# Three edits between attention and ffn_down of a hybrid decoder layer: where the last projections' operands lie, how the sums for ffn_up are formed, in which pieces the residual is loaded

## The chip, the core and the metric

The kernel runs on one core of a Trainium2 chip as one program. Its time is the device time of one launch in microseconds (us), smaller is better. TensorE (PE) multiplies into PSUM, VectorE (DVE) and ScalarE (ACT) read PSUM and SBUF, GpSimd (POOL) reads SBUF, and SyncE (SP) issues every transfer from its one queue, in order. Each engine works through its own list of instructions in order and waits at semaphores for the others.

## What is computed

One decoder layer over 1024 tokens of width 1024 in float32, cut here to the parts that the change touches:

```python
x = x + jnp.concatenate([o_nsa, o_gdn], axis=-1) @ w_out[l]
h = rmsnorm(x, norm_ffn[l])
u = causal_dwconv(h @ ffn_up[l], ffn_conv[l])
gate, up = jnp.split(u, 2, axis=-1)
x = x + (jax.nn.silu(gate) * up) @ ffn_down[l]
return rmsnorm(x, norm_final)
```

o_nsa comes from sparse attention (8 heads, 2 key heads), o_gdn from a gated delta rule (4 heads of 128). ffn_up is 1024 x 5632, ffn_down 2816 x 1024.

## The kernel before

**Numbers.** Every float32 operand of a matmul is split into a high part (an ACT copy to fp32r) and a low part (the operand minus the high part, on DVE or POOL), and a product is three matmuls: high x high, high x low, low x high. The moving operand is 128x512, one PSUM bank.

**Order of work.** The whole program is unrolled. A planner walks it with its own estimate of times and lays out one list for each engine: of what is ready it takes what comes first in the text, unless `tc.issue_after` ties an instruction behind another of its engine. So instructions stand in the lists in another order than in the text, and the lists of a changed kernel can differ far from the change. Tiles lie in pools. Pools are stacked from the left or the right end of SBUF in the order in which they are opened; a pool that comes to lie over bytes of closed pools waits until all users of these pools are done, or, with `reuse_waits="tile"`, each tile waits only for the tiles whose bytes it takes. Inside a pool a tag has `bufs` buffers that are used in turn.

**Phases.** `phase_in` (norm, input projections, the gated delta rule; its last projections are those of `evac_k`, whose split weights lie in pool wk). `phase_attend` runs attention in 16 units, one for each of 8 tiles of 128 tokens (order 7, 6, ..., 0) and 2 key heads: `select` (tile pc), `scores` (tiles p_win and p_sel), `values` (transposes pt, operands ph and pl, sums po), one unit in each of three stages at a time; between their steps the matmuls of `out_gdn` and `out_nsa` are woven in as fillers. `out_gdn` multiplies o_gdn with its half of w_out for all tiles, adds x and stores to x1 in DRAM (d_x1). `out_nsa` does the other half for the four tiles 7 to 4 that are finished early; its operands are the two buffers of tag mg in pool og (mg holds high and low part side by side, 8 KB for two; og's own tag 4 KB). `nsa_norm` norms a finished tile into K.mix.

**`phase_out`** (lines 1020 to 1054) goes over tiles 7 to 4, whose x1 is loaded again (line 1033), and 3 to 0, whose projection is still to be done: the cast mh (line 1037), the low part ml on DVE (line 1040), the residual x_res (line 1042), 24 matmuls out_ps into two banks, the sum with x_res (line 1048), a store. mh, ml and x_res lie in pool xo, which takes bytes of attention's pools. After the first four tiles `norm_transpose` norms and transposes the rows, 32 transposes in eight groups k, and `put_parts` writes the high and low part of group k: D[0] for k below 4, D[1] above.

**`norm_second`** (lines 1063 to 1124) does the same for tiles 3 to 0. ffn_up is computed with Winograd's form of Strassen's product: seven quarter products for eight, with sums of quarters. With the activations' quarters A11 = D[0], A12 = D[1] (the first half of tiles), A21 and A22 = D[2] (the second half), T[2] = A22 - A21, T[0] = A21 - A11 and T[1] = A22 - A21 + A11, T[3] = A12 - T[1]. `put` forms A22 - A21 (s1) in one step of DVE that reads PSUM (line 1102); `late` forms the others out of the split parts, two adds of DVE for each sum (lines 1089 and 1090: 16 adds of 128x512), and splits each (lines 1084 and 1085; POOL does the low parts of T[2] and T[0], DVE those of T[1]). b12 and s1 lie in pool sums.

**`phase_up`**: the first two feature tiles (`plain`) use the eight plain products and run while the sums are made; from the third on `seven` does the seven products, with weights prepared by `prepare` (loads into K.wr and fw2, line 1148, sums of quarters, line 1167, splits, lines 1154 and 1156). Its third product is the first that needs a weight sum (tile ss) and T[1]. Pool fw2 is opened after `late` and takes bytes of sums. `convolve` and `put_away` finish a feature tile and store it to d_a.

**`phase_down`** (lines 1283 to 1410) is Winograd's form too: seven products over the quarters b11, b21, b12, b22 of the weight, each in six steps `pairs`; a step loads a_raw (line 1315), splits it, and issues two more transfers of `queue` behind that load (`fetch`, lines 1306 to 1309). The queue holds b11 and b21 (12 transfers), then the eight rows of x1 (tile x, 0.5 MB each), then b12 and b22. `add` adds a product's two PSUM tiles to a quarter of x. Products 2 to 5 need sums of b12, b22, b11 and b21 (line 1335).

Of the kernel before, what the change touches and what calls it, by code (L numbers as in the profile page):

```python
# [18 lines left out]
P = 128  # L19
# [957 lines left out]
def phase_attend(K, ctx):  # L977
    nc, tc = K.nc, K.tc
    mk = lambda n, b, **kw: ctx.enter_context(tc.tile_pool(name=n, bufs=b, **kw))
    for n in ("apl", "an", "aps", "asm", "ap", "og"):  # L980
        setattr(K, n, mk(n, 2 if n == "asm" else 1, side="right"))
# [38 lines left out]
def phase_out(K):  # L1020

    nc, tc, A = K.nc, K.tc, K.A
    with ExitStack() as st:
        xp = st.enter_context(tc.tile_pool(name="xo", bufs=2, side="right"))
        po = st.enter_context(tc.tile_pool(name="po4", bufs=4, space=PSUM))
        px = st.enter_context(tc.tile_pool(name="pn2", bufs=4, space=PSUM))
        ws = K.ws
        for b, tiles in HALVES:
            for i in tiles:
# [5 lines left out]
                mh = xp.tile([P, 4, P], F32R, name="mh", tag="mh")  # L1035
                ml = xp.tile([P, 4, P], F32R, name="ml", tag="ml")
# [13 lines left out]
            if b:  # L1050
                norm_transpose(K, tiles, lambda j: K.x1[j],
                               lambda k, ps: put_parts(K, *K.D[k // 4][k % 4], ps,
                                                       K.vec[:, V_NFFN + k:V_NFFN + k + 1]), K.fw, px, "px", 4,
                               lambda j: row_tile(K, 4 + j))


def row_tile(K, j):

    n = ("ga", "f_g", "f_u", "ga", "f_g", "f_u", "ga", "acc")[j]
    return K.fw.tile([P, 2 + SEQ], F32, name=n, tag=n, bufs={"ga": 3, "acc": 1}.get(n, 2))[:, 2:]  # L1060


def norm_second(K):
# [6 lines left out]
    K.T = [None] * 4  # L1070

    for j in (1, 2, 0, 3):
        h3 = K.late_pools.enter_context(tc.tile_pool(name=f"h3{j}", bufs=1))
        K.T[j] = [tuple(h3.tile([P, 512], F32R, name=f"t{n}{j}{k}") for n in "hl") for k in range(4)]
# [12 lines left out]
    def add(out, x, j, k, op0, op1):  # L1087

        nc.vector.tensor_tensor(out=out, in0=x, in1=K.D[j][k][0].bitcast(F32), op=op0)
        nc.vector.tensor_tensor(out=out, in0=out, in1=K.D[j][k][1].bitcast(F32), op=op1)  # L1090

    def put(k, ps):
        g = K.vec[:, V_NFFN + k:V_NFFN + k + 1]
        if k < 4:
            put_parts(K, *K.T[3][k], ps, g)
            b12[k] = scr("b12", 4)
            nc.scalar.activation(b12[k], ps, AF.Copy, scale=g)
            return
        k -= 4
        put_parts(K, *K.D[2][k], ps, g)  # L1100
        s2 = s1[k] = scr("s1", 4)
        nc.vector.scalar_tensor_tensor(out=s2, in0=ps, scalar=g, in1=b12[k], op0=ALU.mult, op1=ALU.subtract)
# [3 lines left out]
    def late():  # L1106
        for k in range(4):
            split(2, k, s1[k])
            add(b12[k], b12[k], 0, k, ALU.subtract, ALU.subtract)
# [437 lines left out]
```

## Time and profile before

| | |
|---|---|
| runs | 1497.18, 1500.30, 1500.89 us, median 1500.3 |
| the profiled execution | 1502.3 us, span of the trace 1500.5 us |
| busy share of the span | PE 95%, weight loads 78%, DVE 77%, ACT 48%, POOL 38% |
| matmuls | 7260 |
| a_raw loads of 0.5 MB | 35, median 3.6 us from issue to landing |
| DMA share from 1342 us to the end | 0.35 |

The rows further down come from one profiled execution on the core. Times are in us from the start of the span, unless a line says ns. A row of the waits says which engine's line waited for which engine's line. A timeline's row gives start, length, engine, line, operation, output and inputs; in brackets stands the idle time of that engine before the instruction and what ended it.

### The profile page before, as it was taken

The page shows a single profiled execution, that of the slowest core. Times are in us where ns is not written, and L with a number is a line of the kernel's source. Part 1 is how long each engine was busy: PE and PEld are TensorE (multiplying, and loading weights), DVE is VectorE, ACT ScalarE, POOL GpSimd, SP SyncE. Part 2 cuts the span into 40 slices and gives each one's busy share as a digit, 9 for nine tenths or more (in the row PEclk, how much of TensorE's full clock was granted, in tenths as well). Part 3 has the DMA queues.
Part 4 walks back from the last instruction along what each step waited for, and adds up shares of the span by engine and source line. Part 5 has one row for each costly group of instructions (what it writes and reads, how often), then busy time and mean ns, then how long its engine had stood idle before and what let it go on. Part 6 is the DMA issues. An engine that isn't in the chain of part 4 may idle for free.

```text
span 1500.5 us, 21074 instructions
## 1 busy us (share of the span) xinstructions
PE 1420.9 (95%) x7260; PEld 1163.8 (78%) x7260; DVE 1153.7 (77%) x2222; ACT 723.3 (48%) x1405; POOL 575.3 (38%) x567
## 2 busy tenths in 40 slices
PE   8998899999989999989998979999999999989997
PEld 8876677787877777777787858888888888778886
DVE  5768997886335788898975797888888888687656
ACT  7443343232233566788865544444444445333333
POOL 3355433344352245466563541111111112364444
PEclk9999999999999999999999989999999999999999
DMA  6245352444366543132215112323222235773333
GB/s 234 87 156 177 107 169 72 125 121 150 93 219 173 161 138 112 58 85 52 55 64 200 40 70 105 105 105 106 105 94 98 97 105 194 268 267 87 103 106 147
DMA packets 106059, 188.04 MB, mean 125 GB/s; under 512 B 17216, under 2 KB 52064, under 8 KB 105952
## 3 DMA queue, kind: packets, MB, share of 16 engines
q1 hardware_dynamic: 105952, 186.69, 38.5%
q8 instruction: 57, 0.93, 0.3%
q14 instruction: 50, 0.41, 0.1%
HBM read 135.00 MB, written 51.66 MB: 124 GB/s over the span
## 4 chain that ended last, share of the span: by engine, by line
PE 64%; DVE 19%; DMA 6%; ACT 4%; issue 4%; POOL 2%; SPq 1%; DVEq 0%; ACTq 0%; POOLq 0%
PE up_ps L1130 27%; PE dn_ps L1328 11%; PE proj_ps L128 3%; PE proj_ps L126 3%; PE proj_ps L127 3%; DVE cv_acc L465 3%; PE pt L880 2%; DVE pl L890 2%; PE po L892 1%; DVE zb L350 1%; PE po L891 1%; DVE ztmp L348 1%; PE s_ps L820 1%; PE s_ps L415 1%; DMA d_x<-og 1%
## 5 line engine op out<-in xcount | busy, mean ns | idle before, releaser
L1328 PE MATMUL dn_ps<-d_op 128*128 128x512 f32 x924 | 211.4, 390 | 5.7 <-DVE d_op L1322 3.8
L1328 PEld LDWEIGHTS dn_ps<-d_op 128*128 128x128 f32 x924 | 173.0, 188 | 43.6 <-DVE d_op L1322 5.0
L128 PE MATMUL proj_ps<-hH,w_l 128*128 128x512 f32 x384 | 158.3, 412 | 6.6 <-POOL w_l L118 6.6
L126 PE MATMUL proj_ps<-hH,w_h 128*128 128x512 f32 x384 | 156.2, 408 | 5.0 <-ACT cv_acc L463 3.2
L127 PE MATMUL proj_ps<-hL,w_h 128*128 128x512 f32 x384 | 155.3, 405 | 0.1
L1320 POOL TENSOR_TENSOR d_op<-a_raw,d_op 128x1024 fp32r<-128x1024 f32 (+1 forms) x42 | 104.7, 2496 | 123.0 <-ACT d_op L1319 105.6
L1130 PE MATMUL up_ps<-th,op_h 128*128 128x512 f32 x336 | 133.5, 398 | 7.1 <-ACT op_h L1154 7.1
L1130 PE MATMUL up_ps<-th,op_l 128*128 128x512 f32 x336 | 133.6, 398 | 3.6 <-DVE op_l L1156 3.6
L1130 PE MATMUL up_ps<-tl,op_h 128*128 128x512 f32 x336 | 133.3, 397 | 0.0
L118 POOL TENSOR_TENSOR w_l<-w_raw,w_h 128x1024 fp32r<-128x1024 f32 (+2 forms) x46 | 110.1, 2398 | 46.1 <-ACT w_h L116 44.5
L1322 DVE TENSOR_TENSOR d_op<-b,d_op 128x1024 fp32r<-128x1024 f32 (+1 forms) x42 | 80.8, 1928 | 48.5 <-ACT d_op L1321 42.1
L1130 PE MATMUL up_ps<-dl,op_h 128*128 128x512 f32 x288 | 113.8, 395 | 0.0
L1130 PE MATMUL up_ps<-dh,op_h 128*128 128x512 f32 x288 | 112.6, 395 | 1.0 <-ACT acc L167 1.0
L1130 PE MATMUL up_ps<-dh,op_l 128*128 128x512 f32 x288 | 110.5, 394 | 0.0
L882 ACT ACTIVATE ph<-pt 128x512 fp32r<-128x512 f32 (+1 forms) x148 | 85.3, 591 | 49.1 <-PE pt L880 41.3
L1242 DVE SCALAR_TENSOR_TENSOR ga<-f_g,vec,ga 128x1024 f32<-128x1024 f32 x44 | 89.3, 2029 | 16.9 <-ACT ga L1240 16.3
L890 DVE TENSOR_TENSOR pl<-pt,ph 128x512 fp32r<-128x512 f32 x132 | 89.5, 683 | 9.1 <-ACT ph L882 8.6
L128 PEld LDWEIGHTS proj_ps<-hH,w_l 128*128 128x128 f32 x384 | 74.6, 194 | 26.9 <-POOL w_l L118 10.6
L1154 ACT ACTIVATE op_h<-w_raw 128x1024 fp32r<-128x1024 f32 (+1 forms) x64 | 59.0, 923 | 74.8 <-PE up_ps L1130 69.7
L1319 ACT ACTIVATE d_op<-a_raw 128x1024 fp32r<-128x1024 f32 (+1 forms) x42 | 41.4, 988 | 108.7 <-PE dn_ps L1328 53.8
L1175 POOL MEMSET f_u<- 128x2 f32 x22 | 2.2, 100 | 234.0 <-DVE acc L1242 233.1
L126 PEld LDWEIGHTS proj_ps<-hH,w_h 128*128 128x128 f32 x384 | 74.6, 195 | 21.2 <-ACT cv_acc L463 4.9
(343 smaller groups left out, 3654.6 us busy)
## 6 DMA issues: line engine op xcount, KB each, us to landing
w_raw<-in_w_up_dram SPq DMA_DIRECT2D x44, 512.0 KB, 3.2
a_raw<-d_a SPq DMA_DIRECT2D x35, 512.0 KB, 3.6
w_raw<-in_w_gdn_dram SPq DMA_DIRECT2D x24, 512.0 KB, 3.5
d_a<-ga SPq DMA_DIRECT2D x44, 256.0 KB, 2.0
b<-in_w_down_dram SPq DMA_DIRECT2D x20, 512.0 KB, 6.9
d_a<-so SPq DMA_DIRECT2D x33, 256.0 KB, 2.0
qT<-d_q SPq DMA_DIRECT2D x32, 256.0 KB, 4.8
mg<-d_mix SPq DMA_DIRECT2D x16, 512.0 KB, 3.7
```

Source lines behind the costliest of these rows:

```text
L118: (low or nc.gpsimd).tensor_tensor(out=wl, in0=raw, in1=wh.bitcast(F32), op=ALU.subtract)
L126: nc.tensor.matmul(out, ah, bh, start=(i == 0), stop=False)
L127: nc.tensor.matmul(out, ah, bl, start=False, stop=False)
L128: nc.tensor.matmul(out, al, bh, start=False, stop=(i == n - 1))
L882: nc.scalar.activation(ph[0:kk], pt[0:kk], AF.Copy)
L890: nc.vector.tensor_tensor(out=pl, in0=pt, in1=ph.bitcast(F32), op=ALU.subtract)
L1130: mm = lambda a, b, start, stop: nc.tensor.matmul(out, a, b, start=start, stop=stop, skip_group_check=not first)
L1154: nc.scalar.activation(h, src, AF.Copy)
L1242: nc.vector.scalar_tensor_tensor(out=a, in0=raw[:, j:j + SEQ], scalar=tap(j), in1=a, op0=ALU.mult, op1=ALU.add)
L1320: nc.gpsimd.tensor_tensor(out=al, in0=raw, in1=ah.bitcast(F32), op=ALU.subtract)
L1322: nc.vector.tensor_tensor(out=bl, in0=b[js.start], in1=bh.bitcast(F32), op=ALU.subtract)
L1328: one = lambda a, b, start, stop: nc.tensor.matmul(ps, a, b, start=start, stop=stop, skip_group_check=not first)
```

## The change

Pool og is opened in `tile_hymba` beside K.mix and wn, ahead of attention's pools, and closed with them after `phase_out`; mh and ml of the last four tiles are the two halves of a buffer of mg. The two PSUM pools of `phase_out` wait by tile. In the first half's norm a third ACT copy b11 of each of the first four groups is kept in float32, in the low tiles of T[1] (pool h31, opened earlier). `put` then forms T[0]'s source t0 and T[1]'s source (in b12) with steps of DVE that read PSUM, t0 in the high tiles of T[2]; `late` only splits, in the order T[1], T[0], T[2]. In `phase_down` the residual is loaded in eight transfers of two rows by 512 columns: two of the first quarter at place 6 of the queue, the other six at its end.

```diff
-    for n in ("apl", "an", "aps", "asm", "ap", "og"):
+    for n in ("apl", "an", "aps", "asm", "ap"):
         setattr(K, n, mk(n, 2 if n == "asm" else 1, side="right"))
...
-        po = st.enter_context(tc.tile_pool(name="po4", bufs=4, space=PSUM))
-        px = st.enter_context(tc.tile_pool(name="pn2", bufs=4, space=PSUM))
+        po = st.enter_context(tc.tile_pool(name="po4", bufs=4, space=PSUM, reuse_waits="tile"))
+        px = st.enter_context(tc.tile_pool(name="pn2", bufs=4, space=PSUM, reuse_waits="tile"))
...
-                mh = xp.tile([P, 4, P], F32R, name="mh", tag="mh")
-                ml = xp.tile([P, 4, P], F32R, name="ml", tag="ml")
+                mg = K.og.tile([P, 4, 2 * P], F32R, name="mg", tag="mg", bufs=2)
+                mh, ml = mg[:, :, 0:P], mg[:, :, P:2 * P]
...
-                norm_transpose(K, tiles, lambda j: K.x1[j],
-                               lambda k, ps: put_parts(K, *K.D[k // 4][k % 4], ps,
-                                                       K.vec[:, V_NFFN + k:V_NFFN + k + 1]), K.fw, px, "px", 4,
-                               lambda j: row_tile(K, 4 + j))
+                def put(k, ps):
+                    g = K.vec[:, V_NFFN + k:V_NFFN + k + 1]
+                    put_parts(K, *K.D[k // 4][k % 4], ps, g)
+                    if k < 4:
+                        nc.scalar.activation(K.b11[k], ps, AF.Copy, scale=g)
+                norm_transpose(K, tiles, lambda j: K.x1[j], put, K.fw, px, "px", 4, lambda j: row_tile(K, 4 + j))
...
+def sum_tile(K, j, k, part, dtype=F32R):
+    return K.h3[j].tile([P, 512], dtype, name=f"t{part}{j}{k}", tag=f"{part}{k}")
...
-    for j in (1, 2, 0, 3):
-        h3 = K.late_pools.enter_context(tc.tile_pool(name=f"h3{j}", bufs=1))
-        K.T[j] = [tuple(h3.tile([P, 512], F32R, name=f"t{n}{j}{k}") for n in "hl") for k in range(4)]
+    for j in (2, 0, 3):
+        K.h3[j] = K.late_pools.enter_context(tc.tile_pool(name=f"h3{j}", bufs=1))
+    parts = lambda j: [(sum_tile(K, j, k, "h"), sum_tile(K, j, k, "l")) for k in range(4)]
+
+    t0 = [sum_tile(K, 2, k, "h", F32) for k in range(4)]
+    K.T[3] = parts(3)
...
-    def add(out, x, j, k, op0, op1):
-
-        nc.vector.tensor_tensor(out=out, in0=x, in1=K.D[j][k][0].bitcast(F32), op=op0)
-        nc.vector.tensor_tensor(out=out, in0=out, in1=K.D[j][k][1].bitcast(F32), op=op1)
-
     def put(k, ps):
         g = K.vec[:, V_NFFN + k:V_NFFN + k + 1]
+        diff = lambda out, x: nc.vector.scalar_tensor_tensor(out=out, in0=ps, scalar=g, in1=x, op0=ALU.mult, op1=ALU.subtract)
         if k < 4:
             put_parts(K, *K.T[3][k], ps, g)
             b12[k] = scr("b12", 4)
             nc.scalar.activation(b12[k], ps, AF.Copy, scale=g)
+            diff(t0[k], K.b11[k])
             return
         k -= 4
         put_parts(K, *K.D[2][k], ps, g)
-        s2 = s1[k] = scr("s1", 4)
-        nc.vector.scalar_tensor_tensor(out=s2, in0=ps, scalar=g, in1=b12[k], op0=ALU.mult, op1=ALU.subtract)
+        s1[k] = scr("s1", 4)
+        diff(s1[k], b12[k])
+        diff(b12[k], t0[k])
...
     def late():
-        for k in range(4):
-            split(2, k, s1[k])
-            add(b12[k], b12[k], 0, k, ALU.subtract, ALU.subtract)
-            split(0, k, b12[k])
-            add(s1[k], s1[k], 0, k, ALU.add, ALU.add)
-            split(1, k, s1[k])
+        for j, src in ((1, b12), (0, t0), (2, s1)):
+            K.T[j] = parts(j)
+            for k in range(4):
+                split(j, k, src[k])
         st.close()
...
-    queue = [(t[js.start], src) for t, js, src in b[0] + b[1]] + [(xr[:, i], K.d_x1[i]) for i in range(NT)]
+    res = lambda r, c: [(xr[:, i:i + 2, 512 * c:512 * c + 512],
+                         K.d_x1[i:i + 2, :, 512 * c:512 * c + 512].rearrange("i p c -> p i c"))
+                        for i in (4 * r, 4 * r + 2)]
+    queue = [(t[js.start], src) for t, js, src in b[0] + b[1]]
+    queue[6:6] = res(0, 0)
     queue += [(t[js.start], src) for p in zip(b[2], b[3]) for t, js, src in p]
+    queue += res(1, 0) + res(1, 1) + res(0, 1)
...
             K.wn = mix.enter_context(tc.tile_pool(name="wn", bufs=2, side="right"))
+            K.og = mix.enter_context(tc.tile_pool(name="og", bufs=1, side="right"))
...
+        K.T = [None] * 4
+        K.h3 = {1: mk("h31")}
+
+        K.b11 = [sum_tile(K, 1, k, "l", F32) for k in range(4)]
         phase_out(K)
```

## Rows read from the trace of the kernel before

**Rows 1.** Waits of PE, 784 to 892 us: total, times, longest.

```profile
PE up_ps L1130 <- ACT op_h L1154: 7.1, 1, 7.1
PE up_ps L1130 <- DVE op_l L1156: 3.6, 1, 3.6
PE out_ps L126 <- ACT mh L1037: 2.9, 1, 2.9
```

**Rows 2.** Stretches: length, busy us (instructions) by engine, granted clock, DMA share, GB/s.

```profile
471.70:790.40 318.70, 297.00 (x1723) 245.36 (x1721) 271.21 (x901) 224.59 (x573) 158.56 (x229) 0.98 0.33 96
...
793.28:797.01 3.73, 3.73 (x10) 2.91 (x11) 1.66 (x2) 0.47 (x1) 1.03 (x2) 0.55 0.96 356
...
841.00:888.00 47.00, 36.32 (x154) 28.66 (x152) 47.00 (x48) 24.07 (x35) 28.45 (x19) 0.90 0.09 34
875.90:892.30 16.40, 5.72 (x13) 3.97 (x13) 16.40 (x13) 6.96 (x9) 12.57 (x7) 0.59 0.17 62
...
888.00:1269.00 381.00, 381.00 (x1631) 308.82 (x1632) 320.18 (x332) 176.18 (x216) 64.31 (x60) 0.99 0.30 106
1296.00:1342.00 46.00, 40.32 (x175) 32.06 (x174) 34.02 (x21) 17.69 (x18) 21.07 (x9) 1.00 0.90 330
```

**Rows 3.** Waits of PE in ffn_down, 1296 to 1345 us.

```profile
PE dn_ps L1328 <- DVE d_op L1322: 3.8, 2, 2.9
```

**Rows 4.** Timelines of PE, ACT, DVE; transposes from the chain.

```profile
789.45 0.39 PE L128 MATMUL og_ps<-w_h,mg 128*128 128x512 f32 x1
...
792.62 1.14 ACT L1037 ACTIVATE mh<-mix 128x512 fp32r<-128x512 f32 x2
...
809.54 1.75 PE nt_ps L147 x16
...
809.84 0.69 DVE L1040 TENSOR_TENSOR ml<-mix,mh 128x512 fp32r<-128x512 f32 x1 [1.38 <-ACT mh L1037]
...
820.67 0.39 PE L128 MATMUL out_ps<-w_h,ml 128*128 128x512 f32 x1
```

**Rows 5.** Adds: durations (ns min/median/max) by line; timelines of DVE and ACT.

```profile
L1089 DVE TENSOR_TENSOR b<-b,dh x4: 674/1058/1774, 843.6 to 850.4; 128x512 f32<-128x512 f32 x4
L1089 DVE TENSOR_TENSOR s<-s,dh x4: 676/1228/1785, 846.9 to 856.7; 128x512 f32<-128x512 f32 x4
...
L1102 DVE SCALAR_TENSOR_TENSOR s<-nt_ps,vec,b x4: 735/742/742, 840.3 to 845.6; 128x512 f32<-128x512 f32 x4
...
843.60 1.44 DVE L1089 TENSOR_TENSOR b<-b,dh 128x512 f32<-128x512 f32 x1
...
859.62 3.49 DVE L1090 TENSOR_TENSOR s<-s,dl 128x512 f32<-128x512 f32 x2
...
816.59 2.01 ACT L1154 ACTIVATE op_h<-w_raw 128x1024 fp32r<-128x1024 f32 x2 [3.10 <-PE out_ps L128]
...
839.64 0.75 DVE L188 SCALAR_TENSOR_TENSOR dl<-nt_ps,vec,dh 128x512 fp32r<-128x512 f32 x1 [5.50 <-ACT dh L187]
```

**Rows 6.** Wait of SP's queue, timeline of DVE, GpSimd's splits (ns).

```profile
SPq L1148 <- DVE tl L1085: 40.3, 1, 40.3
...
875.51 1.58 DVE L1167 TENSOR_TENSOR ss<-w_raw 128x512 f32<-128x512 f32 x1
...
885.71 2.11 DVE L1156 TENSOR_TENSOR op_l<-ss,op_h 128x1024 fp32r<-128x1024 f32 x1
...
L1085 POOL TENSOR_TENSOR tl<-s,th x4: 1299/1454/1751, 841.9 to 847.1; 128x512 fp32r<-128x512 f32 x4
```

**Rows 7.** Timeline of SP's queue, and a transfer from the chain.

```profile
1297.83 3.23 SPq L1308 DMA_DIRECT2D x<-d_x  x6
...
1301.15 9.56 DMA a_raw<-d_a
```

**Rows 8.** Start of attention: timelines of DVE and SP's queue, wait of SP.

```profile
466.27 0.23 DVE L750 CUSTOM_DVE_ANT_0 pc<-sc_ps,cat 128x64 f32<-128x64 f32 x1 [7.36 <-PE sc_ps L745]
...
471.74 0.33 SPq L946 DMA_DIRECT2D mg<-d_mix  x1
...
SPq L946 <- PE proj_ps L128: 12.5, 1, 12.5
```

More of the change, by code (lines that the diff above doesn't have):

```diff
@@ L1060, in row_tile @@
     return K.fw.tile([P, 2 + SEQ], F32, name=n, tag=n, bufs={"ga": 3, "acc": 1}.get(n, 2))[:, 2:]
+def sum_tile(K, j, k, part, dtype=F32R):
+    return K.h3[j].tile([P, 512], dtype, name=f"t{part}{j}{k}", tag=f"{part}{k}")
 def norm_second(K):
     nc, tc = K.nc, K.tc
-    K.T = [None] * 4
-    for j in (1, 2, 0, 3):
-        h3 = K.late_pools.enter_context(tc.tile_pool(name=f"h3{j}", bufs=1))
-        K.T[j] = [tuple(h3.tile([P, 512], F32R, name=f"t{n}{j}{k}") for n in "hl") for k in range(4)]
+    for j in (2, 0, 3):
[3 more added lines that the diff above has]
+    K.T[3] = parts(3)
     K.us = K.late_pools.enter_context(tc.tile_pool(name="us", bufs=4, side="right"))
```

## The prediction

> **What bounds the kernel now.** I read the waits of TensorE first. It is busy for 95% of the span (the table above), so a change off its path can only give back TensorE's idle time or its time at half clock. In the stages that the diff touches there are three such places. Between attention and the last projections one wait of 2.9 us on the cast mh [rows 1], and behind it a stretch of 3.73 us with a granted clock of 0.55 [rows 2]. At the start of ffn_up two waits of 7.1 and 3.6 us on the operands of the third product of `seven` [rows 1]. In ffn_down TensorE is idle for 5.7 us between 1296 and 1342 [rows 2], the longest wait 2.9 [rows 3]. Then I read what stands behind each: the engines around the out projections [rows 4], the adds of `late` and what holds VectorE [rows 5], the load and the operand behind them [rows 6], and the transfers of ffn_down [rows 7]. Last I asked what comes after: from 888 to 1269 us TensorE is busy for 381.00 of 381 us, 1631 matmuls at 0.233 each [rows 2], so time that is won before 888 isn't lost again there, as long as that stage is fed as it is now.
>
> **Part 1, the operands of the last projections.** Today mh and ml of tile 3 lie in pool xo, over bytes of attention's pools, and the cast runs at 792.62 [rows 4], behind attention's last writes. After the change they lie in `mg`, which stays open. Its two buffers were last read by tiles 5 and 4 of `out_nsa`; the last of those matmuls begins at 789.45 [rows 4], and tile 5's buffer is free 24 matmuls, 5.6 us, earlier. So the cast can run beside attention's tail, and with PSUM waiting by tile TensorE goes on where attention stops. At most this gives the wait, 2.9, and the slow stretch: its ten matmuls begin over 3.73 us, at full clock over 9 x 0.233 = 2.1, so 1.6. Together 4.5. What is late next is tile 0: its mix comes from the norm of attention's last unit, and its ml ends at 809.84 + 0.69 = 810.5 [rows 4]. Its 24 matmuls take 5.6, 16 transposes that sit between them 1.75, and the last one begins at 820.67 [rows 4], so TensorE gets to tile 0 at about 813.6 now and would at 809.1 then, 1.4 too early. That bounds the gain to 3.1 from below if the norm's chain keeps its times; but two of its steps are small matmuls in TensorE's own queue, which move with it. If only the wait goes and the clock drops all the same, it is 2.9. I take 4.0, nearer to the upper end because the chain moves with the queue.
>
> **Part 2, the sums for ffn_up.** Removed are the 16 adds of lines 1089 and 1090 on VectorE. The first begins at 843.60, the last two end at 863.1 [rows 5]; in between lie one dl and one s of 0.74 each, so the adds hold VectorE for 18.0 us. VectorE is busy for all 47.00 us from 841 to 888 [rows 2]. Added are eight `diff`, the form of line 1102, 0.74 each [rows 5]. The four for t0 come where VectorE has sat idle for 5.50 us [rows 5] and cost nothing (3.0 if that cover is gone), the four for b12 come on the saturated stretch, 3.0. Also added are four ACT copies b11, a 128x512 read of PSUM with a scale, at most 0.74 each by the VectorE form of the same shape, 3.0 in all; ACT has a hole of 3.10 before 816.59 [rows 5], in just that place. So cost 0, bounded by 3.0. Net VectorE is ahead by 18.0 - 3.0 = 15.0 us. The low part of the third product's operand, which ends at 885.71 + 2.11 = 887.8 [rows 6], would be done at 872.8, while TensorE wants it at about 876.5, two matmuls after the third product's start at 875.9. The load in front of it is held on SP for 40.3 us until `tl` of line 1085 is done, because pool fw2 lies over the pool sums, and the subtraction that needs this load begins at 875.51 [rows 6]. After the change sums is free once GpSimd has split T0 and T2, eight times 1.3 to 1.75 us [rows 6] from about 842, with one other step between: 855 to 859, so the load is there by 863 and not by 875.5. The stretch from 875.90 to 892.30 holds 13 matmuls [rows 2], 3.0 us of work, and loses 13.4. I take 12.0 of it, because a margin of 3.7 us on a queue in a new order is seldom kept everywhere; bounds 5 and 13.4. Both chains move with part 1, so that takes nothing from this.
>
> One pair of rows speaks for a smaller gain. The adds of one shape took 0.67 to 1.78 us, the form that reads PSUM never over 0.742 [rows 5], with GpSimd at work beside both. [...]
>
> **Part 3, the residual by quarters.** Today eight loads of 0.5 MB go out from 1297.83, and a load of a_raw behind them at 1301.15 takes 9.56 us [rows 7]; the last quarters of the weight (b12, b22) queue behind too, and VectorE's sums of them pile up before the longest wait, 2.9 us [rows 3]. After the change one MB of residual and one of b12 and b22 go in that place; the other three MB of residual move behind b12 and b22, into a stretch with a DMA share of 0.35 (the table). Six larger or equal issues replace eight on SP. So a_raw lands some 6 us earlier (9.56 against a median of 3.6, the table), and the sums can start in VectorE's holes after 1297. Of 5.7 us I expect all but the 0.9 of the other VectorE wait (3.8 in two times, 2.9 the longer [rows 3]), which hangs on a load that SP issues behind stores of ffn_up, and a little more: 4.5, bounds 0 and 5.7. The later quarters are needed a product or more after their loads, in a stretch where TensorE doesn't wait for them.
>
> **Part 4, a pool that moves.** `og` is now opened ahead of attention's other pools, so these move by 12 KB, and the last of them is `ap` (pc, p_win) where it was `og`. The bytes at that end belonged to pool wk until the last projection: the first load of mg waited 12.5 us on SP for that matmul and went out at 471.74, while pc, in other bytes, began at 466.27 after a hole of VectorE [rows 8]. So pc of the first unit now waits until 471.7. Behind it in VectorE's queue stand p_win and the scores of unit 0. The cost lies between 0 and 5.4 us, and no trace shows it. VectorE has 47 us of holes in the 318.7 of attention [rows 2] to take it up, and TensorE has out_gdn's matmuls to fill with. The order of the whole stage is also planned anew, which may give something. I take 2.0, bounds -2 and 5.4.
>
> **The sum.** The profiled execution took 1502.3 us (span 1500.5): 1502.3 - 4.0 - 12.0 - 4.5 + 2.0 = 1483.8. The median of the runs is 2.0 lower than that execution, so 1481.8, in round figures 1482. With all upper ends it is 1475; with part 1 at 2.9, part 2 at 5, part 3 at 0 and attention at 5.4 it is 1498, but these need not meet.
>
> **Rivals.** (a) The stretch on VectorE moves instead of going. At 0.68 each the 16 adds are 10.9, not 18.0; then VectorE is ahead by only 7.9, op_l is done at 879.9, 3.4 late, and with a slow stretch of 1.6 or more behind it the gain of part 2 is 8 or less: 1486 to 1491. For it: GpSimd's work stays. Against it: its splits come earlier, while VectorE reads PSUM. (b) Part 1 or part 3 doesn't do what it says. With both buffers of mg held to the end, or x1's rows as the next thing that TensorE waits for, part 1 gives 0: 1486. With b12's sums in today's order part 3 gives 0: 1486. With both: 1490. (c) Slower: attention. It runs 318.7 us with TensorE busy for 297.0 and VectorE for 271.2 [rows 2]: 16 units of 19.9 us with 1.4 us of idle TensorE in each, VectorE at 17.0. If the late pc shifts each unit's chain against the fillers, and not the first alone, the stage loses once per unit. From 1.3 us a unit the whole gain is gone; at 1.7 the time is 1482 - 2 + 27 = 1507. Against it: units overlap three deep, so that a single shift is taken up by the holes.
>
> **How the numbers follow.** Forecast (1475 to 1487) 0.60; (a) 0.15; (b) 0.10; (c) 0.07; the rest, 0.08, a mixture of costs that ends between 1490 and 1500. The range 1475 to 1493 holds the forecast, (a) and (b) and a little of the rest. A change of 0.3%, 4.5 us, is about what a measurement of this kernel can tell from none. Faster (under 1495.8): the first three and a part of the rest, 0.86; within 0.3% 0.07; slower 0.07.
>
> **What would show it.** Right: no wait before the first out_ps matmul and a granted clock near 1 there; no wait of TensorE near 876; SP's wait in front of fw2's load ended by GpSimd some 15 us earlier; a_raw after the residual loads landing in under 6 us. Wrong: a wait of TensorE on op_l in the first `seven`, a hole before tile 0's projection, or clearly more than 22 us of idle TensorE in attention. The forecast fails most of all if VectorE's queue in the 40 us after the second transposes is planned so that the operands of the third product come behind the convolutions.

## The result, and the profile after

The changed kernel takes 1486.55 us in the median (1485.21 to 1491.67) beside 1498.74 for the kernel before: a ratio of 0.9924 with a 95% interval of 0.9895 to 0.9953, so 12.2 us (0.8%) faster. Run again beside the experiments it gave 0.9907 (0.9889 to 0.9925). The forecast was 1482, so the direction and the range held, but two thirds of the expected gain came, and not from the places where it was expected. The profiled execution has a span of 1484.2 us, against 1500.5 before.

One table serves for all that follows: from the first and last matmul on out_ps, up_ps and dn_ps in each trace, the time of the first projection of `phase_out`, the length from there to the first matmul of ffn_up ("out"), from there to the last of ffn_up ("up"), and from there to the last of ffn_down ("down"). The ratio is to the kernel before, run beside it.

| kernel | ratio (95%) | first out_ps | out | up | down |
|---|---|---|---|---|---|
| before | | 793.3 | 28.7 | 456.2 | 212.7 |
| changed | 0.9924 (0.9895 to 0.9953) | 785.8 | 25.4 | 451.1 | 212.3 |
| e1, pool alone | 1.0001 (0.9989 to 1.0013) | 788.1 | 28.7 | 456.6 | 214.0 |
| e2, parts 1 and 4 | 0.9993 (0.9980 to 1.0006) | 788.1 | 25.7 | 460.5 | 212.7 |
| e3, part 2 | 0.9962 (0.9945 to 0.9978) | 788.0 | 29.3 | 450.4 | 214.1 |
| e4, part 3 | 0.9992 (0.9978 to 1.0006) | 791.2 | 28.7 | 456.5 | 212.3 |
| e5, changed again | 0.9907 (0.9889 to 0.9925) | 788.2 | 25.3 | 450.4 | 212.6 |
| e6, T[3]'s sums left out | 0.987 (0.9848 to 0.9892) | 791.6 | 25.4 | 442.7 | 212.4 |
| e7, sums tied back | 0.9959 (0.9941 to 0.9976) | 785.5 | 25.4 | 451.1 | 218.3 |
| e8, T[3] from PSUM | 0.9938 (0.9918 to 0.9958) | 791.6 | 25.4 | 454.6 | 213.2 |
| e9, low parts on VectorE | 0.9875 (0.9854 to 0.9895) | 787.7 | 25.3 | 445.3 | 212.2 |
| e10, two sums a step | 0.991 (0.9887 to 0.9933) | 788.5 | 25.3 | 451.3 | 210.0 |
| e11, GpSimd doesn't read | 0.9853 (0.983 to 0.9876) | 786.0 | 25.4 | 443.8 | 212.1 |
| e12, both on VectorE | 0.9842 (0.982 to 0.9864) | 789.6 | 25.3 | 443.9 | 205.7 |

The reader should first see how far each column can be trusted. Before and e4 share everything up to ffn_down: first out_ps 793.3 and 791.2, but out 28.7 twice and up 456.2 and 456.5. Changed and e5 are one kernel: 785.8 and 788.2, out 25.4 and 25.3, up 451.1 and 450.4. All that lies ahead of `phase_out` so moves by some us from one execution to the next, and the lengths of out and up by less than 1 (down by somewhat more, see e1 and e3). Of the 16.3 us between the two spans, 7.4 lie ahead of the first out_ps, and only the wait of 2.9 us in them is the change's; the rest is that scatter, since e1, which has the same pools in attention, gains nothing.

Where the time went: the waits of TensorE from 784 to 892 us in the changed kernel (engine and line that waited, what it waited for, total, times, longest), which answer to [rows 1].

```profile
PE up_ps L1135 <- ACT op_h L1159: 2.2, 1, 2.2
PE up_ps L1135 <- DVE f_g L1172: 1.0, 1, 1.0
PE up_ps L1135 <- DVE op_l L1161: 0.7, 1, 0.7
PE up_ps L1135 <- POOL op_l L1161: 0.6, 1, 0.6
```

The wait on mh is gone, 7.1 and 3.6 have become 0.7 on op_l, and three waits that the kernel before doesn't have stand behind it. Where they stand, on TensorE's timeline (start, length, instruction, idle time before it and its releaser):

```profile
785.50 0.50 PE L892 MATMUL po<-pl,vst 128*128 128x512 f32 x1
785.84 0.39 PE L126 MATMUL out_ps<-w_h,mg 128*128 128x512 f32 x1
...
866.80 0.50 PE L1135 MATMUL up_ps<-th,op_l 128*128 128x512 f32 x1 [0.69 <-DVE op_l L1161]
...
874.35 0.50 PE L1135 MATMUL up_ps<-dh,op_h 128*128 128x512 f32 x1 [2.17 <-ACT op_h L1159]
...
876.04 0.58 PE L1135 MATMUL up_ps<-dh,op_h 128*128 128x512 f32 x1 [0.95 <-DVE f_g L1172]
...
877.66 0.79 PE L1135 MATMUL up_ps<-dh,op_l 128*128 128x512 f32 x1 [0.61 <-POOL op_l L1161]
```

The stretches that answer to [rows 2] (length, busy time and instructions of PE, weight loads, DVE, ACT and POOL, granted clock, DMA share, GB/s):

```profile
785.84:811.24 25.40, 25.40 (x130) 21.42 (x128) 13.72 (x25) 13.15 (x23) 8.13 (x13) 1.00 0.50 180
865.40:883.97 18.57, 14.15 (x45) 9.91 (x45) 18.57 (x18) 8.41 (x11) 7.78 (x6) 0.82 0.23 71
874.35:883.28 8.93, 7.37 (x18) 5.01 (x18) 8.93 (x8) 3.98 (x6) 3.45 (x4) 0.62 0.02 7
1280.10:1326.10 46.00, 41.23 (x175) 33.38 (x174) 38.71 (x26) 15.85 (x17) 19.92 (x8) 0.96 0.85 311
...
886.00:1250.00 364.00, 364.00 (x1569) 295.13 (x1568) 304.20 (x316) 169.30 (x206) 60.08 (x56) 1.00 0.30 104
```

The out projections run without a gap (25.40 of 25.40 us) and at a granted clock of 1.00. From 865.40 to 883.97 the 45 matmuls take 18.57 us where 45 x 0.233 = 10.5 would do: 8.1 are lost, half in waits and half at a granted clock of 0.62, against 13.4 before. The 46 us of ffn_down in [rows 2] begin 15.9 us earlier here. They have 4.8 us of idle TensorE, against 5.7: nearly all in one wait of 4.4, where there were four waits. But the granted clock is 0.96 there and was 1.00, and the same 175 matmuls keep TensorE busy for 41.23 us where it was 40.32: what the waits gave, the clock took. After 886 TensorE is never idle until ffn_down (364.00 of 364.00 us to 1250), as before.

### The profile page after: what moved, and what is told of

The parts are those of the page before. It is cut to its first block, busy times and chain, and to the rows that moved or that the text cites. A ratio compares the mean times of both kernels' runs of the same rounds, so it can differ in the third digit from the quotient of the medians.

```text
span 1484.2 us, 21079 instructions
## 1 busy us (share of the span) xinstructions
PE 1419.2 (96%) x7260; PEld 1163.0 (78%) x7260; DVE 1146.3 (77%) x2214; ACT 724.5 (49%) x1409; POOL 570.7 (38%) x567
## 4 chain that ended last, share of the span: by engine, by line
PE 66%; DVE 19%; DMA 5%; ACT 4%; issue 3%; POOL 2%; SPq 1%; DVEq 0%; ACTq 0%; POOLq 0%
PE up_ps L1135 27%; PE dn_ps L1338 11%; DVE cv_acc L465 3%; PE proj_ps L128 3%; PE proj_ps L126 3%; PE proj_ps L127 3%; PE pt L880 2%; DVE pl L890 2%; PE po L892 2%; PE po L891 1%; DVE zb L350 1%; PE s_ps L820 1%; DVE ztmp L348 1%; PE s_ps L415 1%; PE s_ps L822 1%
## 5 line engine op out<-in xcount | busy, mean ns | idle before, releaser
L1247 DVE SCALAR_TENSOR_TENSOR ga<-f_g,vec,ga 128x1024 f32<-128x1024 f32 x44 | 89.5, 2035 | 12.3 <-ACT ga L1245 11.7
```

What stands on the lines that cost most here:

```text
L1247: nc.vector.scalar_tensor_tensor(out=a, in0=raw[:, j:j + SEQ], scalar=tap(j), in1=a, op0=ALU.mult, op1=ALU.add)
```

## The experiments

**The parts alone.** Each is made on the kernel before. e1 opens og early and leaves mh and ml in xo:

```diff
-    for n in ("apl", "an", "aps", "asm", "ap", "og"):
+    for n in ("apl", "an", "aps", "asm", "ap"):
...
+            K.og = mix.enter_context(tc.tile_pool(name="og", bufs=1, side="right"))
```

e2 adds part 1 to it, so that it is parts 1 and 4:

```diff
+        po = st.enter_context(tc.tile_pool(name="po4", bufs=4, space=PSUM, reuse_waits="tile"))
+        px = st.enter_context(tc.tile_pool(name="pn2", bufs=4, space=PSUM, reuse_waits="tile"))
...
+                mg = K.og.tile([P, 4, 2 * P], F32R, name="mg", tag="mg", bufs=2)
+                mh, ml = mg[:, :, 0:P], mg[:, :, P:2 * P]
```

e3 is part 2 with its pools and tiles, at its core

```diff
+                    if k < 4:
+                        nc.scalar.activation(K.b11[k], ps, AF.Copy, scale=g)
...
+            diff(t0[k], K.b11[k])
...
+        diff(s1[k], b12[k])
+        diff(b12[k], t0[k])
```

and e4 is part 3:

```diff
+    queue[6:6] = res(0, 0)
...
+    queue += res(1, 0) + res(1, 1) + res(0, 1)
```

> The kernel before with one edit: pool og is opened ahead of attention's pools and stays open; mh and ml stay in xo. This is part 4 alone. The prediction puts its cost at 2.0 us (between a gain of 2 and a loss of 5.4): ratio to the kernel before 1.001, and pc of the first unit would begin about 5 us later, at 471 to 472 us, with more than 22 us of idle TensorE in attention. What the trace of the changed kernel suggests instead (first matmul on s_ps 2.1 us earlier, last one 4.3 us earlier): attention gets 2.2 us shorter, ratio 0.9985. Third reading: the 2.2 us come from another part of the change, by the new plan of the lists, and this kernel takes the time of the kernel before within 1 us.

> The kernel before with parts 1 and 4 alone: og kept open, mh and ml as halves of mg, PSUM of the last projections waiting by tile. The prediction: 2.0 - 4.0 = 2.0 us gained, ratio 0.9987, the first projection of tile 3 directly behind attention, tile 0 as the next late thing. The trace of the changed kernel suggests 2.2 + 6.6 = 8.8 us gained up to the first matmul of ffn_up; if ffn_up then starts earlier but its third product is still late by its own chain on VectorE, a part of this is lost again at 876 us, where the wait of 7.1 us on op_h would be up to 8.8 us longer. So 8.8 us gained (ratio 0.994) if VectorE's chain moves with it, near 0 (ratio 0.999 to 1.0) if it does not.

> The kernel before with part 2 alone: sums for ffn_up from PSUM. The prediction: 12.0 us gained (5 to 13.4), ratio 0.992, no wait of TensorE at the third product of the first feature tile by seven products. The trace of the changed kernel suggests 4.9 us: the wait of the third product falls to 0.7 us, and the operands of the next feature tile are late instead, by 2.2 + 0.9 + 0.6 us of waits and some twenty matmuls at half clock; ratio 0.9967.

> The kernel before with part 3 alone: residual by quarters. The prediction: 4.5 us gained (0 to 5.7), ratio 0.997. The trace of the changed kernel suggests 0.4 us, because a wait of 4.4 us on VectorE's low part takes the place of four shorter ones: ratio 0.9997, and in the trace one wait of 4 to 5 us on d_op some 15 us after the first product's add to the residual.

Measured: the ratios and lengths in the table. The pool costs nothing that can be seen. In e2, part 1 wins its 2.9 us of waiting and 3.0 in out, and loses 4.3 of them in up. The wait where they go, on e2's timeline, and then the four longest of e3's five waits from 780 to 900 us:

```profile
879.63 0.80 PE L1130 MATMUL up_ps<-th,op_h 128*128 128x512 f32 x1 [11.80 <-ACT op_h L1154]
```

```profile
PE up_ps L1135 <- DVE f_g L1172: 3.4, 1, 3.4
PE out_ps L126 <- ACT mh L1038: 2.9, 1, 2.9
PE up_ps L1135 <- ACT acc L167: 1.6, 1, 1.6
PE up_ps L1135 <- ACT f_u L1175: 1.5, 1, 1.5
```

In e2 the wait of 7.1 on op_h has grown to 11.8: TensorE wants the operand 8.1 us earlier on the trace's clock (867.8 for 875.9), and gets it only 3.4 us earlier (879.63 for 883.09); VectorE's first add begins 5.6 earlier (838.01 for 843.60). In e3 the operands of the third product are in time, the wait on mh is still there, and the release of PSUM banks is late: 3.4 us for the step of VectorE that adds a bank to f_g, 1.5 and 0.6 (the fifth wait) for copies on ACT. So part 1 needs part 2: alone they give 0.07% and 0.38%, and all parts together 0.8% (0.9% in e5). In up the changed kernel is 9.4 us shorter than e2, only 5.1 shorter than before, and about as short as e3, so the gain of part 1 in out is kept beside part 2. Down is less steady: 212.7 to 214.1 in the four executions with the old order of the residual, 212.1 to 213.2 in the seven with the new one alone. Their means, 213.4 and 212.4, give part 3 about 0.9 us; the two profiled executions of before and changed give 0.4.

**What is late behind the third product.** e6 drops the twelve adds for T[3]:

```diff
-            w = row_tile(K, 0)[:, 0:512]
-            src = [t.bitcast(F32) for t in (K.D[1][k][0], *K.T[1][k], K.D[1][k][1])]
-            nc.vector.tensor_tensor(out=w, in0=src[0], in1=src[1], op=ALU.subtract)
-            nc.gpsimd.tensor_tensor(out=w, in0=w, in1=src[2], op=ALU.subtract)
-            nc.vector.tensor_tensor(out=w, in0=w, in1=src[3], op=ALU.add)
             with tc.issue_after(gps.ins):
-                split(3, k, w)
+                split(3, k, K.D[1][k][0].bitcast(F32))
```

e8 keeps them in value but forms them ahead of the stretch, from A12 + (A21 - A11) and one step that reads PSUM:

```diff
             diff(t0[k], K.b11[k])
...
+            for part in K.D[1][k]:
+                nc.vector.tensor_tensor(out=w3[k], in0=t0[k] if part is K.D[1][k][0] else w3[k], in1=part.bitcast(F32), op=ALU.add)
             return
...
         diff(b12[k], t0[k])
+        nc.vector.scalar_tensor_tensor(out=w3[k], in0=ps, scalar=ng[:, k:k + 1], in1=w3[k], op0=ALU.mult, op1=ALU.add)
```

> The changed kernel itself, with more runs, beside the experiments that start from it. The first four runs gave a ratio of 0.9924 to the kernel before; the sum of the parts alone (1.0001, 0.9993, 0.9962, 0.9992) gives 0.995 if the parts only add up. If part 1's gain is kept only together with part 2, as the traces suggest (part 1 alone: 6 us won up to ffn_up, 4.3 us of it lost again at the third product), the ratio stays near 0.992 to 0.993.

> The changed kernel with the twelve adds for T[3] left out (T[3] is split from the high part of D[1], so this part of the sum isn't computed): eight adds on VectorE, four on GpSimd. Theory A: what is late at 872 us is this chain (VectorE, GpSimd, VectorE, then ScalarE's copy and GpSimd's split), which stands in all three queues in front of the split of the next feature tile's weights. Then the waits of 2.2, 0.9 and 0.6 us and the slow stretch behind them go, up to 8 us: ratio 0.987 to 0.988. Theory B: the late thing is the load of the weights or the release of PSUM banks by convolve; then the waits stay and the time stays within 2 us of the changed kernel.

> The changed kernel with the source of T[3] formed earlier: A12 + (A21 - A11) by two adds of VectorE in the transposes of the first four groups, then one step that reads A22 from PSUM with the negative gain; the twelve adds behind them go. Eight two-input adds move from the saturated stretch after 842 us to the one before it, four steps of 0.74 us come, four adds of GpSimd go. Theory A (the chain for T[3] is late): up to 8 us less than the changed kernel, ratio to the kernel before 0.987 to 0.988. Theory C (the new steps delay the split parts that ffn_up needs first): waits of TensorE between 825 and 845 us, and a time above the changed kernel's.

Measured: without the adds, up is 442.7, 7.7 to 8.4 less than in the changed kernel, and from 780 to 920 us TensorE has this one wait, in the norm of attention's last unit:

```profile
PE nrm_ps L918 <- POOL sq L915: 0.2, 1, 0.2
```

So what is late at 872 us comes with the adds for T[3]: their chain across the engines, or the time that they take on VectorE and GpSimd, for e6 removes both. In the changed kernel's queues it looks like this: ACT's copy th and POOL's split tl of T[3] stand ahead of op_h and op_l of the next weights, for which TensorE waits at 874.35 and 877.66.

```profile
871.11 1.58 DVE L1126 TENSOR_TENSOR ga<-ga,dl 128x512 f32<-128x512 f32 x1
...
872.72 0.63 ACT L1093 ACTIVATE th<-ga 128x512 fp32r<-128x512 f32 x1 [2.07 <-DVE ga L1126]
873.25 1.04 ACT L1159 ACTIVATE op_h<-w_raw 128x1024 fp32r<-128x1024 f32 x1
...
873.43 1.41 POOL L1094 TENSOR_TENSOR tl<-ga,th 128x512 fp32r<-128x512 f32 x1 [1.29 <-ACT th L1093]
874.79 2.81 POOL L1161 TENSOR_TENSOR op_l<-w_raw,op_h 128x1024 fp32r<-128x1024 f32 x1
```

Yet forming the sums earlier (e8) made up 3.5 to 4.2 us longer. The first 48 us of ffn_up, of the changed kernel and of e8 (columns as above):

```profile
811.24:859.24 48.00, 48.00 (x228) 39.36 (x227) 39.33 (x47) 32.19 (x52) 29.39 (x25) 1.00 0.23 77
```

```profile
817.00:865.00 48.00, 46.80 (x222) 37.96 (x220) 44.03 (x51) 33.23 (x54) 31.40 (x25) 1.00 0.16 55
```

VectorE is busy for 4.7 us more there, and from 832.7 to 885.7 us it has no hole. The waits come on op_h (4.9 us in two, 4.0 the longer) and on f_g (1.2), though not between 825 and 845 us, where theory C had put them. Moved work isn't saved work. VectorE's time isn't the only possible cause: the load into fw2, which SP issues once the last `tl` has freed pool sums, goes out at 864.30 in e8 and at 847.01 in the changed kernel, 11.5 us later when both are counted from the first matmul of ffn_up. Which of the two makes the waits isn't separated.

**Why VectorE is short of time.** e9 gives VectorE sixteen steps that GpSimd had:

```diff
-        (nc.vector if j == 1 else nc.gpsimd).tensor_tensor(out=l, in0=src, in1=h.bitcast(F32), op=ALU.subtract)
+        nc.vector.tensor_tensor(out=l, in0=src, in1=h.bitcast(F32), op=ALU.subtract)
...
-            nc.gpsimd.tensor_tensor(out=w, in0=w, in1=src[2], op=ALU.subtract)
+            nc.vector.tensor_tensor(out=w, in0=w, in1=src[2], op=ALU.subtract)
```

e11 leaves VectorE's steps as they are and lets GpSimd write zeros in place of its low parts and of its weight splits up to the fourth feature tile, and drops its subtraction for T[3]:

```diff
+        if j == 1:
+            nc.vector.tensor_tensor(out=l, in0=src, in1=h.bitcast(F32), op=ALU.subtract)
+        else:
+            nc.gpsimd.memset(l.bitcast(F32), 0.0)
...
-            nc.gpsimd.tensor_tensor(out=w, in0=w, in1=src[2], op=ALU.subtract)
...
+        if eng is nc.gpsimd and K.f < 4:
+            K.last_split = eng.memset(l.bitcast(F32), 0.0)
...
```

> The changed kernel with the low parts of T[0], T[2], T[3] and the middle subtraction for T[3] on VectorE instead of GpSimd: sixteen steps of 128x512 more on VectorE. Theory A (two engines share a way into SBUF): in the trace of the changed kernel a two-input step of 128x512 takes 0.68 us when GpSimd rests and about 1.57 beside it; each GpSimd step of 1.3 to 1.6 us so costs VectorE about 0.9, more than the 0.68 of doing it itself. Then VectorE's steps from 842 to 870 us take 0.68, the stretch does not get longer for it, the waits behind the third product shrink, and ffn_up is 0 to 5 us shorter (ratio to the kernel before 0.988 to 0.991). Theory B (VectorE's time adds up, GpSimd's work costs it nothing): 16 x 0.68 = 10.9 us more on a saturated engine, ffn_up 5 to 11 us longer, ratio 0.994 to 0.998.

> The changed kernel in which GpSimd reads nothing at the start of ffn_up: its low parts (of T[0], T[2], T[3], and of the first four feature tiles' weights) are filled with zeros instead of computed, and its subtraction for T[3] is left out. VectorE's list keeps all its steps. Theory A (contention): the two-input steps of VectorE take 0.68 us (128x512) and 1.21 (128x1024) all through 842 to 880 us; about 25 steps there are 0.9 us shorter, VectorE is 10 to 20 us ahead, and the waits behind the third product go: ffn_up 7 to 8.5 us shorter, ratio to the kernel before 0.986 to 0.987. Theory B (the chain across engines for T[3], not VectorE's time): steps of 1.5 us remain, and the gain is below 4 us.

Groups of VectorE's instructions from 842 to 880 us (count, busy us, mean ns), of the changed kernel, of e9 and of e11:

```profile
L1124 DVE TENSOR_TENSOR ga<-dh,th 128x512 f32<-128x512 f32 x4 | 6.7, 1682 | 1.0 <-POOL tl L1094 1.0
L1094 DVE TENSOR_TENSOR tl<-b,th 128x512 fp32r<-128x512 f32 x3 | 4.7, 1613 | 0.0
L1098 DVE SCALAR_TENSOR_TENSOR b<-nt_ps,vec,th 128x512 f32<-128x512 f32 x1 | 0.7, 746 | 0.0
```

```profile
L1094 DVE TENSOR_TENSOR tl<-b,th 128x512 fp32r<-128x512 f32 x4 | 2.7, 686 | 0.0
L1125 DVE TENSOR_TENSOR ga<-ga,tl 128x512 f32<-128x512 f32 x4 | 2.7, 684 | 0.0
L1124 DVE TENSOR_TENSOR ga<-dh,th 128x512 f32<-128x512 f32 x4 | 2.7, 686 | 0.0
```

```profile
L1127 DVE TENSOR_TENSOR ga<-dh,th 128x512 f32<-128x512 f32 x4 | 2.7, 686 | 0.0
```

The same subtraction of dh and th takes 1682 ns beside GpSimd's subtractions, and 686 in e9 and in e11. In these 38 us (columns as above) VectorE gets through 32 instructions in the changed kernel and 47 in e9, busy nearly all the time in both:

```profile
842.00:880.00 38.00, 33.58 (x136) 25.62 (x135) 37.01 (x32) 20.00 (x28) 24.73 (x16) 0.95 0.21 69
```

```profile
842.00:880.00 38.00, 37.45 (x160) 29.73 (x159) 38.00 (x47) 21.64 (x30) 10.26 (x5) 1.00 0.19 70
```

With all sixteen steps on VectorE up is 445.3, 5.1 to 5.8 less than in the changed kernel, and the ratio 0.9875; two waits of 0.3 and 0.2 us are left in ffn_up. Without GpSimd's reads, up to the fourth feature tile, up is 443.8. Theory A's step times hold in both, 0.68 to 0.69 us for 128x512: what GpSimd took off VectorE's list cost VectorE more than it saved. Both runs also take GpSimd's steps out of the chain for T[3], so how much of the gain is the shorter chain isn't shown.

**ffn_down.** The chain behind the wait of the changed kernel at 1310.40: its wait, VectorE's steps ahead of it, and, from the chain of work, the load that the first sum waited for.

```profile
PE dn_ps L1338 <- DVE d_op L1332: 4.8, 2, 4.4
```

```profile
1298.01 9.04 DVE L1345 TENSOR_TENSOR b<-b,b 128x1024 f32<-128x1024 f32 x4
1306.98 3.37 DVE L1332 TENSOR_TENSOR d_op<-b,d_op 128x1024 fp32r<-128x1024 f32 x1
```

```profile
1285.33 9.30 DMA b<-in_w_down_dram
```

e7 ties the sums behind the low parts of the second product's last three steps, e10 two by two. In the diff `lows` lists the instructions that make the low parts of b, product after product; e10 has the index shown, e7 has 6 + min(pairs.index(js) + 3, 5) in its place. e12 is e9 and e10, and puts the low part of a_raw in the second and third product on VectorE:

```diff
+        with tc.issue_after(lows[8 + pairs.index(js)].ins):
+            comb(b12, b22, b12, ALU.subtract, js)
+            comb(b11, b12, b11, ALU.add, js)
...
-        nc.gpsimd.tensor_tensor(out=al, in0=raw, in1=ah.bitcast(F32), op=ALU.subtract)
+        (nc.vector if n in (1, 2) else nc.gpsimd).tensor_tensor(out=al, in0=raw, in1=ah.bitcast(F32), op=ALU.subtract)
```

> The changed kernel with the sums of b12, b22 and b11 for ffn_down's third product tied on VectorE behind the low parts of the second product's last three steps; the same work in another order. Theory A: the wait of 4.4 us at 1306 us comes from four sums that stand in front of one low part in VectorE's list (9.04 us for the four). Then it goes, and the time falls by 4 to 5 us (ratio to the kernel before 0.989 to 0.990). Theory B: VectorE has too much to do there, at 2.3 us for a sum of 1.2; then the wait comes back at the third product, and the time stays within 1 us or gets worse.

> The changed kernel with the sums of b12, b22 and b11 for ffn_down's third product tied on VectorE two by two behind the low parts, four steps ahead of their use; in the run before them the sums were tied to three steps only, and eight of them then stood in one block of 14.6 us in front of the first low part of the third product. Theory A (the number of sums in front of one low part sets the wait): with two sums between two low parts VectorE needs 2 x 2.3 + 1.2 to 3.4 = 5.8 to 8 us a step where TensorE needs 5.6; with four steps of lead the waits fall under 2 us together, ffn_down is 3 to 4 us shorter than in the changed kernel, ratio to the kernel before 0.988 to 0.989. Theory B (too much work for VectorE at that place, in any order): waits of 4 us and more in all, ratio 0.990 to 0.994.

> The changed kernel with both findings together: the sixteen GpSimd steps for T[0], T[2], T[3] on VectorE as in the run that gave 0.9875, the sums of ffn_down two by two, and the low parts of a_raw in ffn_down's second and third product on VectorE instead of GpSimd. Theory A (in ffn_down too GpSimd's reads stretch VectorE's sums from 1.2 to 2.3 us, so that a step takes 5.8 to 8 us against TensorE's 5.6): without them a step of VectorE is 2 x 1.2 for the two low parts and 2 x 1.2 for the sums, 4.8 us, less than 5.6, and the waits of 1290 to 1340 us, 3.3 to 4.8 together, fall under 1.5: ffn_down 208 to 210 us from the last matmul of ffn_up to its own last (212.3 in the changed kernel), ratio to the kernel before 0.984 to 0.986. Theory B (the late thing there is the load of a_raw and of the weights' quarters, or the round trip over ScalarE): ffn_down 212 us or more, ratio 0.987 to 0.989.

Measured, e7's wait and the block of VectorE that makes it, then e10's wait, then the stretch of ffn_down in e12 with three of VectorE's steps in it:

```profile
PE dn_ps L1340 <- DVE d_op L1334: 10.2, 2, 9.0
```

```profile
1313.54 14.59 DVE L1347 TENSOR_TENSOR b<-b,b 128x1024 f32<-128x1024 f32 x8
```

```profile
PE dn_ps L1340 <- DVE d_op L1334: 3.3, 3, 2.2
```

```profile
1285.00:1335.00 50.00, 50.00 (x222) 41.21 (x221) 40.47 (x38) 20.40 (x22) 0.00 (x0) 1.00 0.77 269
```

```profile
1297.67 1.22 DVE L1347 TENSOR_TENSOR b<-b,b 128x1024 f32<-128x1024 f32 x1
1298.81 1.22 DVE L1332 TENSOR_TENSOR d_op<-a_raw,d_op 128x1024 fp32r<-128x1024 f32 x1
1299.94 1.22 DVE L1347 TENSOR_TENSOR b<-b,b 128x1024 f32<-128x1024 f32 x1
```

Tied to three steps, eight sums pile up in front of one low part and TensorE waits 9.0 us: worse. Two a step leave 3.3 us in three waits, and down is 210.0, 2.3 to 2.6 less, which lies between the two theories; the ratio, 0.991, can't tell it from the changed kernel. Only about 1 us of that is waiting: e5, which is the changed kernel, waits 4.3 us there, 0.4 on GpSimd and the rest on VectorE's low part, so the one wait of 4.4 isn't in every execution. The rest is the clock. From 40 to 60 us behind the last matmul of ffn_up it was granted at 0.91 in e5 and at 1.00 in e10:

```profile
PE dn_ps L1338 <- DVE d_op L1332: 3.9, 3, 2.1
```

```profile
1303.88:1323.88 20.00, 16.27 (x64) 12.66 (x63) 20.00 (x14) 4.85 (x6) 10.20 (x4) 0.91 0.88 305
```

```profile
1305.06:1325.06 20.00, 19.23 (x85) 15.59 (x84) 19.90 (x11) 6.95 (x8) 13.98 (x5) 1.00 0.86 303
```

With GpSimd still (e12), VectorE's sums take 1.22 us instead of 9.04 / 4 = 2.26, TensorE is busy for 50.00 of 50 us, and down is 205.7. So with two sums a step and GpSimd still nothing is late, and the loads of a_raw and b, which theory B named, are in time. No run has GpSimd still in the old order, so what the order adds isn't shown. e12 is 1475.95 us in the median beside 1498.28, a ratio of 0.9842: nearly twice as far from the kernel before as the change is.

## Why the prediction was right in direction and wrong in its terms

| step | forecast (bounds) | measured by the lengths |
|---|---|---|
| part 1 | 4.0 gained (2.9 to 4.5) | 6.2 gained: 2.9 of waiting, 3.3 in out |
| part 2 | 12.0 gained (5 to 13.4) | 5.1 gained (9.4 beside part 1) |
| part 3 | 4.5 gained (0 to 5.7) | 0.4 gained (0.9 by the means) |
| part 4 | 2.0 lost (gain of 2 to loss of 5.4) | 0, ratio 1.0001 |
| sum | 18.5 | 11.7 |

**Part 1**: the mechanism was right: the first projection follows attention's last matmul directly, tile 0 doesn't wait, since the norm's chain moved with TensorE's queue as argued, though by less: tile 0's low part was done at 804.2, 6.3 us earlier than before, 0.2 ahead of its first matmul at 804.38. Its size passed the upper bound, because the bound took only the wait on mh and the clock behind it. A third loss was in the trace of before and not in the sum: at 822.01 the first matmul of ffn_up waited 0.96 us for a bank (line 167), and this went too:

```profile
822.01 0.47 PE L1130 MATMUL up_ps<-dh,op_h 128*128 128x512 f32 x1 [0.96 <-ACT acc L167]
```

2.9 + 1.6 + 1.0 is 5.5. Of the last 0.7 some 0.4 only changes columns: four of the 32 transposes, 0.11 us each, come behind the first matmul of ffn_up in the changed kernel. The rest I can't put to a row.

**Part 2**: what VectorE gains came true. The first `s` begins at 834.34 where it began at 840.3 [rows 5], 6.0 earlier, and the low part of the third product's operand is done at 865.53 + 1.21 = 866.7 where it was done at 887.8, 21.1 earlier. So VectorE is 15.1 us ahead in its own course, and 15.0 was forecast. SP's wait for fw2, 22.2 us long instead of 40.3, ended at 847.0; with VectorE's 6.0 added that is 853.0, about the 855 to 859 that I put.

The wait of SP's queue, and the timelines of SP and DVE:

```profile
SPq L1153 <- DVE tl L1094: 22.2, 1, 22.2
```

```profile
847.01 0.80 SPq L1153 DMA_DIRECT2D w_raw<-in_w_up_dram  x2
...
834.34 0.74 DVE L1098 SCALAR_TENSOR_TENSOR s<-nt_ps,vec,b 128x512 f32<-128x512 f32 x1
...
865.53 1.21 DVE L1161 TENSOR_TENSOR op_l<-ss,op_h 128x1024 fp32r<-128x1024 f32 x1
```

The first step that failed is "Both chains move with part 1, so that takes nothing from this". TensorE came to the third product at 865.43 where it came at 875.9, 10.5 earlier, and VectorE's chain began only 6.0 earlier. The 4.5 between them took the margin of 3.7, and the operand was 0.7 late. Counted from the first out_ps, the first `s` comes after 47.0 us before, 46.6 in e2 and 48.7 in e3. So part 1 moves it by 0.4 where it moves TensorE by 3.0 (out in e2), and in e2 4.3 us were lost for it. The rest is part 2's own: its added steps, which I had put at 0 with a bound of 3.0, put the first `s` off by 1.7.

The second is the question asked too late. I asked what comes next only from 888 us on, where TensorE is always busy, and took the end of the lost stretch for the end of its cause. The next operand came 7.6 us behind that of the third product, from a chain on the same saturated VectorE, and the stretch still lost 8.1 of the 13.4 that I counted as free.

Rival (a), at 0.15, had the core of this, a stretch that moves on VectorE instead of going; its gain of "8 or less" and its 1486 to 1491 fit better than the forecast's. Its working didn't hold: by it VectorE is 7.9 ahead and the operand 3.4 late, and 15.1 and 0.7 were measured. Its reason, that GpSimd's work stays, was right: in e11, where GpSimd reads nothing at that place, the two-input step of VectorE that took 1682 ns beside GpSimd in the changed kernel takes 686, and the form that reads PSUM took 746 there and 743 in e11. I made the price from the 16 adds alone, and VectorE's other two-input steps of 128x512 were as long: 1613 ns for the low parts of T[1], 1682 for the first step of T[3].

**Part 3**: the sums did start in VectorE's holes, and just that made the wait: four of them, 2.26 us each beside GpSimd, stood in front of a low part that TensorE needed, and that took 3.37 us itself in this execution and 1.21 in e5. That is rival (b) for part 3, for another reason than the one given there. I priced the loads (too short: a_raw issued at 1283.04 landed after 6.9 us and the next one after 10.7, and I had said under 6) and left out what VectorE does with what they bring, and the clock, 0.96 here where it was 1.00. In e12, with VectorE's sums at 1.22 us, this stretch has no wait.

**Part 4**: the step was seen rightly, its price was not. pc began 0.5 us after the last projection (469.2), where it had begun 5.0 before it (471.3); nothing was late for it. DVE's timeline and the wait of SP that answer to [rows 8]:

```profile
469.70 0.23 DVE L750 CUSTOM_DVE_ANT_0 pc<-sc_ps,cat 128x64 f32<-128x64 f32 x1 [3.59 <-PE proj_ps L128]
```

```profile
SPq L946 <- PE proj_ps L128: 12.6, 1, 12.6
```

A wait of an engine that has 47 us of holes in its stage was worth 0, the lower of the plausible values. Rival (c), attention losing in every unit, didn't occur: the first projection begins between 785.5 and 791.6 in the eleven executions with the new pools, and between 788.0 and 793.3 in the three with the old ones, which still have the wait of 2.9 us on mh (as e1 has).

So 1482 was near, and the range held, in part by luck, through errors of both signs: 11.0 us of gain too much in ffn_up and ffn_down (6.9 and 4.1), 4.2 too little in parts 1 and 4 (2.2 and 2.0).

## What to carry to other kernels

When a saturated engine makes TensorE wait, list what stands in its queue behind the wait that you remove, up to the point where the engine has holes again: a gain ends at the next operand, not at the end of the lost stretch. Before giving VectorE's surplus to GpSimd, compare the two-input steps of VectorE that run beside GpSimd with those that run alone; here they took 1.6 to 1.7 us beside it and 0.68 to 0.69 without its reads, and taking the work back was the faster choice: e9's median is 4 us below that of the changed kernel (e5), and that of e12, which does it in ffn_down too and sets the sums two by two, 10. The lengths of out and up tell 1 us apart where medians of whole runs tell 3.

## What the runs showed of the hardware

Beside GpSimd's subtractions, which took 1.1 to 2.1 us for 128x512 (one took 3.74) and 2.8 for 128x1024, two groups of two-input steps of VectorE of 128x512 took 1613 and 1682 ns in the mean in the changed kernel; with GpSimd's reads left out (e11) they took 683 and 686. VectorE does the subtractions of GpSimd itself in 0.68 to 0.69 us (e9; one took 2.30). A memset of GpSimd (128x1024, 0.96 us from 846.07 in e11) left the steps of VectorE beside it at 0.69 or less. GpSimd's own steps differ too: its subtraction of 128x1024 took 2.81 us at 874.79 in the changed kernel, and in e8 two of its instructions, that subtraction among them, held it for 8.66 us between 875 and 890; what made them longer isn't shown. Behind a wait of TensorE of 2.2 us, and with waits of 1.0 and 0.6 inside, the granted clock was 0.62 over 8.93 us (the stretch from 874.35). In e9, with waits of 0.3 and 0.2 us at that place, it was 1.00 over 18.50 us:

```profile
867.20:885.70 18.50, 17.95 (x77) 13.88 (x76) 18.41 (x22) 8.48 (x12) 5.06 (x3) 1.00 0.23 86
```
